# q and k heads transposed in pairs in float32 and split on the way out of PSUM; dilated groups projected in class order

## The chip, the core and the metric

The kernel runs on one core of one Trainium2 chip. The metric is the device time of one execution in microseconds. Three runs of the kernel before took 1957.49, 1953.87 and 1952.23 us: median 1953.87 us. The engines are PE (TensorE, with its weight loads shown apart as PEld), DVE (VectorE), ACT (ScalarE), POOL (GpSimd) and SP (SyncE, which here only issues DMAs).

## What is computed

Two layers of a decoder trunk over 512 tokens with 1024 features. In each layer the normed residual goes through one wide projection, which feeds four mixers of attention (A: sparse by an indexer's top 128, B: dilated windows in three groups, C: latent attention, D: a banded window with sinks); each mixer's output is gated, projected and summed, and added to the residual. What the change touches is the way from the projection to the attention of A, B and D:

```
qa = rms_norm(a_q.reshape(shp_a), qk_gain_a[l, 0])
ka = rms_norm(a_k.reshape(shp_a), qk_gain_a[l, 1])
...
B_GROUPS = ((128, 1), (512, 4), (2048, 16))
...
def to_sub(t):
    t = t.reshape(b, sub_len, dil, h, dh).transpose(0, 2, 1, 3, 4).reshape(b * dil, sub_len, h, dh)
...
s = jnp.einsum('bnqkgd,bnskd->bnkgqs', qb, kb, preferred_element_type=jnp.float32) * dh ** -0.5
```

Each head of q and of k (64 features) is divided by its root mean square over the features and multiplied by a gain. Groups 1 and 2 of mixer B attend among tokens of the same residue mod 4 (a "class" of 128 tokens) or mod 16. All of it is float32 in the reference.

## The kernel before

**Exact products.** Matmuls take `F32R` operands, which hold a rounded part of a float32. So each operand is two tiles, `hi` (a rounded copy) and `lo` (the rest), and each product is three passes: hi by hi, hi by lo, lo by hi. Weights stream through SP in slots of up to 128x768 (L402), ACT makes `hi` (L405) and DVE `lo` (L411).

**Projection.** `t_bank` fills one PSUM bank with 128 tokens by the columns of a pair of heads: for 8 tiles of the contraction 3 passes each (L512, L513, L514), 24 matmuls; the stationary operand is the activation (128x128), the moving one the weights. `f_bank` gives features by 512 tokens, with the weights stationary (L536 to L538), 512 columns a matmul.

**A pair of heads** (`do_pair`; 4 in A, 12 in B per layer, of which 8 are of groups 1 and 2, `perm`; `do_d` makes one such pair in `d0` and six more q heads in `d1`, from one normed bank of 384 columns per token tile). For each of four token tiles: a bank of 384 columns (q, k, v of two heads); v is split from PSUM into `vv`; `norm_qk` copies q and k out (`evac`, L642), squares (ACT L651), sums (DVE L653), takes the power -1/2 (POOL L378, L379), multiplies (DVE L657), applies the product of both gains to k (POOL L659), and writes `hi` (POOL L660) and `lo` (DVE L661) of each head side by side, 128 columns of F32R. After two token tiles `q_out` and `k_out` transpose each head by itself (L676, L689: 4 q and 4 k transposes of 128x128, in F32R), so that `hi` comes to lie in 64 partitions over `lo` in the other 64, and ACT copies them to the feature-major tiles `uq` and `kk(h, 0)` (L680 to L696). `k_swap` (L701, L702) then has four DMAs, issued by POOL, make `kk(h, 1)` with `lo` over `hi`. A score block is one matmul of 128 partitions with each of the two.

**Class order.** Pairs of groups 1 and 2 need their tokens sorted by class. Before, q and k are projected in token order (banks of 256 columns) and sorted by ACT as it copies them out of the transposes (L680, L693 write with a step of 128 elements). v is projected apart as one `f_bank` of 24 matmuls of 512 columns, sorted in ACT's copy to `vp` (L734), transposed back by four float32 transposes (L737) and split.

**Order of work.** `PLAN` lists pieces (pairs, attentions, gate projections `z`, merges) in order of preference; a list scheduler fixes each engine's order from it, so that banks of later pieces fill PE while an attention waits. Each engine then runs its list strictly in order. At the start, SP also writes the bias tables: `gdram` (L338), and from it copies in DRAM (`make_skew`, L347) that later loads (L372) read shifted.

Of the kernel before, what the change touches and what calls it, by code (L numbers as in the profile page):

```python
# [112 lines left out]
def plan():  # L113
    """The order of a layer's work; what comes first is preferred where several pieces are ready."""
# [127 lines left out]
def build(ctx, tc, A, depth=2, dump=None):  # L242
# [132 lines left out]
    def rsqrt(eng, r, ss, n, scale, eps=EPS):  # L375
        """r = 1 / sqrt(ss * scale + eps) on [128, n]."""
# [5 lines left out]
    def layer(l, xt):  # L382
# [8 lines left out]
        gv = lay[:, 728:920].rearrange("p (i d) -> p i d", i=3)  # L391
        sy.dma_start(pk, A["pk"][l][:, :PK])
# [22 lines left out]
        def gain_parts():  # L415
            """x * gain as hi and lo per row tile: the first products need not wait for the norm."""
# [50 lines left out]
        pg = T([128, 512], F32, "tmp")[:, :384].rearrange("p (i j d) -> p i j d", i=3, j=2)  # L467
        with tc.issue_after(wdma[0].ins):
            sy.dma_start(pg.rearrange("p i j d -> p (i j d)"), A["pk"][l][:, PK:])
        ve.scalar_tensor_tensor(gv, pg[:, :, 0], A_SC, pg[:, :, 1], op0=OP.mult, op1=OP.mult)  # L470
# [33 lines left out]
        def t_bank(slots, w, t, c0=0, c1=None, x=None):  # L504
            c1 = w if c1 is None else c1
# [25 lines left out]
        def f_bank(parts, mh, ml, w=S):  # L531
            """parts: (hi, lo) stationary views [128, 128] per row tile; moving operands mh, ml: [128, w] each."""
# [11 lines left out]
        def split_ps(hi, lo, src, scale=None):  # L544
            """hi + lo = src (* scale), src in PSUM."""
# [92 lines left out]
        def evac(o, n, scale=1.0):  # L638
            """A copy of a bank's first n columns, so that the bank is free before the norms are known."""
# [7 lines left out]
        def norm_qk(o, t, x, gi, scale=1.0):  # L647
            """o: two heads of q and of k in PSUM; hi and lo of the normed ones to x[:, t], [128, 4, 2, 64]."""
            o = evac(o, 256, scale)
            sq = T([128, 512], F32, "ssq")[:, :256]  # L650
            ac.activation(sq, o, AF.Square)  # L651
            ss = T([128, 8], F32, "nss")[:, :4]
            ve.tensor_reduce(ss, sq.rearrange("p (h d) -> p h d", h=4), axis=AX.X, op=OP.add)  # L653
            r = T([128, 8], F32, "nr")[:, :4]
            rsqrt(gp, r, ss, 4, 1.0 / 64)
# [13 lines left out]
        def q_out(uq, qx, hf, h0, n, perm):  # L669
            """Heads of qx [128, 2, n, 2, 64] (half hf of the tokens) to uq[:, h0:h0 + n], feature-major."""  # L670
            for i0 in range(0, n, 2):
                m = min(2, n - i0)
                p = ps_t(F32R)
                for i in range(m):
                    for t in range(2):
                        pe.transpose(p[:, (2 * i + t) * 128:(2 * i + t + 1) * 128], qx[:, t, i0 + i], idr)  # L676
                src = p[:, :m * 256].rearrange("p (h s) -> p h s", h=m)
                if perm:
                    dst = uq[:, h0 + i0:h0 + i0 + m].rearrange("p h (c i) -> p h i c", c=4)[:, :, hf * 64:hf * 64 + 64]
                    ac.copy(dst, src.rearrange("p h (i c) -> p h i c", c=4))  # L680
                else:
                    ac.copy(uq[:, h0 + i0:h0 + i0 + m, hf * 256:hf * 256 + 256], src)

        def k_out(kk, x, hf, perm):
            """The two k heads of x (half hf of the tokens), hi on top of lo, to kk(h, 0)."""
            p = ps_t(F32R)
            for i in range(2):
                for t in range(2):
                    pe.transpose(p[:, (2 * i + t) * 128:(2 * i + t + 1) * 128], x[:, t, 2 + i], idr)  # L689
            for i in range(2):  # L690
                src = p[:, i * 256:(i + 1) * 256]
                if perm:
                    ac.copy(kk(i, 0).rearrange("p (c i) -> p i c", c=4)[:, hf * 64:hf * 64 + 64],  # L693
                            src.rearrange("p (i c) -> p i c", c=4))
                else:
                    ac.copy(kk(i, 0)[:, hf * 256:hf * 256 + 256], src)  # L696
# [10 lines left out]

        def do_pair(job):
# [5 lines left out]
            vv = u4().rearrange("p a b -> p (a b)").rearrange("p (t h d) -> p t h d", t=NT, h=2)  # L714
            for t in range(NT):
                if t % 2 == 0:
                    x = T([128, 2, 4, 2, 64], F32R, "qk")
                o = t_bank(slots, 384, t, 0, 256 if perm else 384)
                if not perm:
                    v = o[:, 256:384].rearrange("p (h d) -> p h d", h=2)  # L720
                    split_ps(vv[:, t, :, 0:64], vv[:, t, :, 64:128], v)
                last = norm_qk(o, t % 2, x, int(br == BR_B))
                if br == BR_B:
                    topk_after(last, TOPK_B[job[2]])
                if t % 2:
                    q_out(uq, x, t // 2, 0, 2, perm)
                    k_out(kk, x, t // 2, perm)
            k_swap(kk)
            if perm:
                o = f_bank([(slots[k // 2][0][:, (k % 2) * 384 + 256:(k % 2) * 384 + 384],  # L730
                             slots[k // 2][1][:, (k % 2) * 384 + 256:(k % 2) * 384 + 384]) for k in range(KT)],
                           xhs, xls)
                vp = T([128, 512], F32, "tmp")
                ac.copy(perm_view(vp, True), nat_view(o, True))  # L734
                p = ps_t()
                for t in range(NT):
                    pe.transpose(p[:, t * 128:(t + 1) * 128], vp[:, t * 128:(t + 1) * 128], idf)  # L737
                pv = p.rearrange("p (t h d) -> p t h d", t=NT, h=2)
                split_ps(vv[:, :, :, 0:64], vv[:, :, :, 64:128], pv)
# [589 lines left out]
```

## Time and profile before

| | |
|---|---|
| median of three runs | 1953.87 us |
| the profiled execution, its span | 1949.2 us |
| PE busy | 1884.5 us, 97% |
| DVE, ACT, POOL busy | 68%, 57%, 37% |
| mean granted TensorE clock | 0.986 of full speed |
| matmuls | 11348 |

The span is that of one profiled execution, from its first to its last instruction; the medians are of whole executions, 4.7 us longer. PE is busy nearly throughout, by a measure in which matmuls overlap: a matmul's own time runs from its start to the end of its results, and the next starts well before. What a matmul costs PE is therefore the distance between starts in a stretch without waits, and that is what the timeline rows below are for. A group's mean in the rows by line is the longer, overlapping time.

### The profile page before, as it was taken

Reading aid. Unit: us, or ns where it says so; the run is one execution under the profiler, and the core shown is the slowest. Engines: PE = TensorE matmul, PEld = TensorE weight load, DVE = VectorE, ACT = ScalarE, POOL = GpSimd, SP = SyncE. Lnnn points to the kernel's source line nnn. Section 1 sums busy time; section 2 is a strip of 40 time slices with the busy share of each in tenths; the row PEclk is TensorE's granted clock in tenths of the full one; section 3 lists DMA queues with packets and bytes.
Section 4 is the critical chain, followed back from the end, with each engine's and each line's share of the span. In section 5 each row is a group of like instructions: output and inputs, shape, how many; then the busy total and the mean of one; then the engine's idle time right before and its main releaser. Section 6 shows DMA issues by size and latency. Waiting matters only on the chain.

```text
span 1949.2 us, 33221 instructions
## 1 busy us (share of the span) xinstructions
PE 1884.5 (97%) x11348; PEld 1695.6 (87%) x11348; DVE 1331.1 (68%) x3410; ACT 1103.0 (57%) x2650; POOL 728.5 (37%) x1186
## 2 busy tenths in 40 slices
PE   8759999999989999999999999999999999999999
PEld 7648889989878998998889988899899989898887
DVE  7649777758476866665469888676768686766542
ACT  6538666656455565554347776566555656555431
POOL 3615353424233346640005345253343343755000
PEclk9879999999989999999999999999999999999999
DMA  4223233342334243332252222233333333333233
GB/s 163 84 91 95 67 90 103 105 113 88 110 105 118 80 121 105 99 98 82 91 187 85 82 66 93 74 88 83 94 105 113 101 101 91 117 96 101 80 92 108
DMA packets 103420, 193.47 MB, mean 99 GB/s; under 512 B 21510, under 2 KB 35924, under 8 KB 103252
## 3 DMA queue, kind: packets, MB, share of 16 engines
q1 hardware_dynamic: 92372, 173.52, 29.4%
q0 software_dynamic: 10880, 17.83, 4.2%
q8 instruction: 90, 1.47, 0.3%
q14 instruction: 78, 0.64, 0.1%
HBM read 168.84 MB, written 12.83 MB: 93 GB/s over the span
## 4 chain that ended last, share of the span: by engine, by line
PE 88%; DMA 4%; DVE 2%; ACT 2%; POOL 2%; issue 1%; SPq 1%; DVEq 0%; ACTq 0%; POOLq 0%
PE acc L537 14%; PE acc L536 14%; PE acc L538 14%; PE acc L512 9%; PE acc L513 9%; PE acc L514 9%; PE S L923 4%; PE T L994 3%; PE T L1014 2%; DMA cbuf<-wall 1%; DMA sd<-st 1%; PE T L1033 1%; PE T L1026 1%; PE T L676 1%; PE T L689 1%
## 5 line engine op out<-in xcount | busy, mean ns | idle before, releaser
L411 DVE TENSOR_TENSOR cbufr<-cbuf,cbufr 128x768 fp32r<-128x768 f32 (+3 forms) x396 | 357.6, 906 | 140.5 <-ACT cbufr L405 139.0
L405 ACT CAST cbufr<-cbuf 128x768 fp32r<-128x768 f32 (+3 forms) x396 | 304.9, 774 | 262.4 <-PE acc L537 195.9
L513 PE MATMUL acc<-cbufr 128*128 128x384 f32 (+1 forms) x1152 | 365.8, 318 | 0.0
L512 PE MATMUL acc<-cbufr 128*128 128x384 f32 (+1 forms) x1152 | 364.1, 317 | 0.0
L514 PE MATMUL acc<-cbufr 128*128 128x384 f32 (+1 forms) x1152 | 363.9, 316 | 0.0
L536 PE MATMUL acc<-cbufr 128*128 128x512 f32 x896 | 354.5, 396 | 0.9 <-ACT raw L642 0.9
L538 PE MATMUL acc<-cbufr 128*128 128x512 f32 x896 | 353.9, 395 | 0.0
L537 PE MATMUL acc<-cbufr 128*128 128x512 f32 x896 | 353.6, 395 | 0.0
L513 PEld LDWEIGHTS acc<-cbufr 128*128 128x128 f32 x1152 | 218.7, 190 | 3.0 <-issue 1.1
L512 PEld LDWEIGHTS acc<-cbufr 128*128 128x128 f32 x1152 | 218.5, 190 | 2.7 <-ACT U L696 0.7
L514 PEld LDWEIGHTS acc<-cbufr 128*128 128x128 f32 x1152 | 218.7, 190 | 2.3 <-issue 0.8
L379 POOL TENSOR_TENSOR nr<-nx,cbuf 128x4 f32<-128x4 f32 (+2 forms) x200 | 211.6, 1060 | 11.1
L538 PEld LDWEIGHTS acc<-cbufr 128*128 128x128 f32 x896 | 168.9, 188 | 34.0
L536 PEld LDWEIGHTS acc<-cbufr 128*128 128x128 f32 x896 | 169.0, 189 | 32.7 <-ACT raw L642 1.3
L537 PEld LDWEIGHTS acc<-cbufr 128*128 128x128 f32 x896 | 169.1, 189 | 32.3 <-issue 0.7
L958 POOL TENSOR_SCALAR P<-P,rd 128x128 f32<-128x128 f32 x192 | 117.3, 621 | 195.4 <-DVE rd L956 136.2
L378 POOL TENSOR_SCALAR nx<-nss 128x4 f32<-128x4 f32 (+2 forms) x200 | 62.3, 311 | 272.2 <-DVE nss L653 243.1
L701 POOL DMA_DIRECT2D U<-U x68 | 39.3, 578 | 311.4 <-ACT U L693 190.4
L547 ACT CAST PT<-T 128x128 fp32r<-128x128 f32 (+2 forms) x224 | 102.9, 478 | 64.0 <-PE T L994 38.0
L548 DVE TENSOR_TENSOR PT<-T,PT 128x128 fp32r<-128x128 f32 (+2 forms) x224 | 119.8, 548 | 22.0 <-ACT PT L547 20.3
L945 ACT ACTIVATE P<-P,nm 128x128 f32<-128x128 f32 x192 | 101.9, 533 | 57.4 <-DVE nm L942 56.7
L642 ACT COPY raw<-acc 128x256 f32<-128x256 f32 (+2 forms) x192 | 70.4, 377 | 107.9 <-PE acc L514 74.9
(256 smaller groups left out, 3954.0 us busy)
## 6 DMA issues: line engine op xcount, KB each, us to landing
cbuf<-wall SPq DMA_DIRECT2D x284, 384.0 KB
cbuf<-wall SPq DMA_DIRECT2D x96, 256.0 KB
U<-U POOLq DMA_DIRECT2D x136, 128.0 KB, 2.8
bias<-skew SPq DMA_DIRECT2D x32, 128.0 KB
bias<-skew SPq DMA_DIRECT2D x16, 256.0 KB
skew<-gdram SPq DMA_DIRECT2D x8, 384.0 KB
cbuf<-wall SPq DMA_DIRECT2D x8, 328.0 KB
skew<-gdram SPq DMA_DIRECT2D x4, 640.0 KB
```

Of the source, the lines that this page charges most:

```text
L379: gp.tensor_tensor(r, y, mhalf[:, :n], op=OP.pow)
L405: pin(ac.copy(h, raw))
L411: pin(e.tensor_tensor(lo, raw, h, op=OP.subtract))
L512: mm(o[:, :c1 - c0], x[kt][:, 0, ts], h[:, a + c0:a + c1], start=kt == 0, stop=False)
L513: mm(o[:, :c1 - c0], x[kt][:, 0, ts], lo[:, a + c0:a + c1], start=False, stop=False)
L514: mm(o[:, :c1 - c0], x[kt][:, 1, ts], h[:, a + c0:a + c1], start=False, stop=kt == KT - 1)
L536: mm(o[:, :w], h, mh[kt], start=kt == 0, stop=False)
L537: mm(o[:, :w], h, ml[kt], start=False, stop=False)
L538: mm(o[:, :w], lo, mh[kt], start=False, stop=kt == n - 1)
L547: ac.copy(hi, src)
L548: ve.tensor_tensor(lo, src, hi, op=OP.subtract)
L958: gp.tensor_scalar(p[:, off:off + nk * 128], p[:, off:off + nk * 128], rd[:, qb:qb + 1], 0.0, op0=OP.mult, op1=OP.add)
```

## The change

**Transposes.** `norm_heads` replaces `norm_qk`: it stops at the multiplied float32 heads `qn` (tile `qh`). After all four token tiles, `heads_out` transposes two heads at once in float32 (L664 of the changed kernel: `qn` of 128 tokens by 2x64 features is one 128x128 transpose), four transposes into one bank, and splits each head's 64 partitions from PSUM: ACT writes `hi`, DVE writes `lo`. For head 0 `hi` lies in partitions 0 to 63 and `lo` in 64 to 127, for head 1 the other way round. k goes first, with its gain as a scale per partition in that split; then `k_swap`; then q. The gain is now a column of `par` (`gk`), computed from the small parameter tile, so POOL's multiplication L659, the DMA L469 of replicated gains and POOL's `hi` L660 are gone. Per pair there are 8 transposes in place of 16; in `d1` 12 in place of 24.

**Class order.** For groups 1 and 2 the stationary operand of `t_bank` is `xperm`: every fourth token of the activation, so a bank holds one class. All three of q, k and v come from banks of 384 columns; the `f_bank` for v, `vp`, its transposes, and ACT's sorting copies are gone. The stationary operand is then read with a step of 4 elements (16 bytes) between columns, in 1536 matmuls.

**Else.** `qn` has 4 buffers in place of 6, a new tag `qh` has 6; the scratch of DMAs that POOL issues is set to 4096.

```diff
-        def norm_qk(o, t, x, gi, scale=1.0):
-            """o: two heads of q and of k in PSUM; hi and lo of the normed ones to x[:, t], [128, 4, 2, 64]."""
-            o = evac(o, 256, scale)
...
-            qn = T([128, 256], F32, "qn").rearrange("p (h d) -> p h d", h=4)
...
-            (gp if GAIN_POOL else ve).tensor_tensor(qn[:, 2:4], qn[:, 2:4], gv[:, gi, None].to_broadcast([128, 2, 64]), op=OP.mult)
-            gp.tensor_scalar(x[:, t, :, 0], qn, 1.0, 0.0, op0=OP.mult, op1=OP.add)
-            return ve.tensor_tensor(x[:, t, :, 1], qn, x[:, t, :, 0], op=OP.subtract)
+        def norm_heads(o, n, scale=1.0):
+
+            o = evac(o, n * 64, scale)
...
+            qn = T([128, 512], F32, "qh")[:, :n * 64].rearrange("p (h d) -> p h d", h=n)
+            ins = ve.tensor_tensor(qn, o.rearrange("p (h d) -> p h d", h=n), r[:, :, None].to_broadcast([128, n, 64]),
+                                   op=OP.mult)
+            return qn, ins
+
+        def heads_out(dst, qns, h0, gain=None):
+
+
+            p = ps_t()
+            for t in range(NT):
+                pe.transpose(p[:, t * 128:(t + 1) * 128], qns[t][:, h0:h0 + 2].rearrange("p h d -> p (h d)"), idf)
+            for h in range(2):
+                a, b = (slice(0, 64), slice(64, 128)) if h == 0 else (slice(64, 128), slice(0, 64))
+                d = dst(h)
+                split_ps(d[a], d[b], p[a], None if gain is None else gain[a])
...
+        xperm = [xhl[:, :, kt].rearrange("p e (i c) -> p e c i", c=4) for kt in range(KT)]
...
+                xs = [xperm[kt][:, e, t] if perm else x[kt][:, e, ts] for e in range(2)]
+                mm(o[:, :w], xs[0], h[:, a:a + w], start=kt == 0, stop=False)
+                mm(o[:, :w], xs[0], lo[:, a:a + w], start=False, stop=False)
+                mm(o[:, :w], xs[1], h[:, a:a + w], start=False, stop=kt == KT - 1)
...
             for t in range(NT):
-                if t % 2 == 0:
-                    x = T([128, 2, 4, 2, 64], F32R, "qk")
-                o = t_bank(slots, 384, t, 0, 256 if perm else 384)
-                if not perm:
-                    v = o[:, 256:384].rearrange("p (h d) -> p h d", h=2)
-                    split_ps(vv[:, t, :, 0:64], vv[:, t, :, 64:128], v)
-                last = norm_qk(o, t % 2, x, int(br == BR_B))
+                o = t_bank(slots, 384, t, perm=perm)
+                v = o[:, 256:384].rearrange("p (h d) -> p h d", h=2)
+                split_ps(vv[:, t, :, 0:64], vv[:, t, :, 64:128], v)
+                qn, last = norm_heads(o, 4)
+                qns.append(qn)
...
-                if t % 2:
-                    q_out(uq, x, t // 2, 0, 2, perm)
-                    k_out(kk, x, t // 2, perm)
+            heads_out(lambda h: kk(h, 0), qns, 2, gk[:, int(br == BR_B):int(br == BR_B) + 1])
             k_swap(kk)
-            if perm:
-                o = f_bank([(slots[k // 2][0][:, (k % 2) * 384 + 256:(k % 2) * 384 + 384],
...
-                vp = T([128, 512], F32, "tmp")
-                ac.copy(perm_view(vp, True), nat_view(o, True))
...
+            heads_out(lambda h: uq[:, h], qns, 0)
             return uq, ks, vv
```

The scheduler's lists move with it. The first place is in PE's list, at the pair of group 2 and the first two heads of mixer B in layer 0: each row is a line, an operation, its output tile and its operands, and xN counts repeats. `acc` is a bank, `T` a bank of transposes or of an attention's output, `U` a tile of q, k or v, `S` scores, `qk` and `qh` the normed heads. Before, PE at the end of that pair's banks:

```order
L514 MATMUL acc_4623<-cbufr 128x256
L512 MATMUL acc_4623<-cbufr 128x256
L971 MATMUL S_4377<-U_984_4131,U_983_4130 128x256 x2
L971 MATMUL S_4386<-U_984_4131,U_983_4130 128x256 x2
L513 MATMUL acc_4623<-cbufr 128x256
L514 MATMUL acc_4623<-cbufr 128x256
L536 MATMUL acc_4683<-cbufr 128x512
L537 MATMUL acc_4683<-cbufr 128x512
L538 MATMUL acc_4683<-cbufr 128x512
```

and the same place now:

```order
L925 MATMUL S_4273<-U_961_4033,U_959_4031 128x256 x2
L510 MATMUL acc_4458<-cbufr 128x384
L511 MATMUL acc_4458<-cbufr 128x384
L512 MATMUL acc_4458<-cbufr 128x384
L534 MATMUL acc_4619<-cbufr 128x512
L535 MATMUL acc_4619<-cbufr 128x512
L536 MATMUL acc_4619<-cbufr 128x512
```

`acc_4683` is the bank of v alone, 24 matmuls of 512 columns; it is gone, the banks of q, k and v are 384 wide, and what follows them (`acc_4619`, a merge) is work that both kernels do. Later in PE's list, the transposes of that same pair, before:

```order
L1026 MATMUL T_4446<-PT_4438,U_986_4133 64x128
L676 MATMUL T_4566<-cbufr,qk_4479 128x128 x4
L689 MATMUL T_4572<-cbufr,qk_4479 128x128 x2
L1026 MATMUL T_4446<-PT_4438,U_986_4133 64x128 x11
L689 MATMUL T_4572<-cbufr,qk_4479 128x128 x2
L676 MATMUL T_4666<-cbufr,qk_4579 128x128 x4
L689 MATMUL T_4672<-cbufr,qk_4579 128x128 x4
L512 MATMUL acc_4915<-cbufr 128x384
```

and now:

```order
L980 MATMUL T_4299<-PT_4291,U_962_4034 64x128
L664 MATMUL T_4500<-cbuf,qh_4369 128x128
L664 MATMUL T_4500<-cbuf,qh_4411 128x128
L664 MATMUL T_4500<-cbuf,qh_4453 128x128
L664 MATMUL T_4500<-cbuf,qh_4495 128x128
L980 MATMUL T_4299<-PT_4291,U_962_4034 64x128 x11
L664 MATMUL T_4513<-cbuf,qh_4369 128x128
L664 MATMUL T_4513<-cbuf,qh_4411 128x128
L664 MATMUL T_4513<-cbuf,qh_4453 128x128
L664 MATMUL T_4513<-cbuf,qh_4495 128x128
```

Sixteen transposes became eight, k's four ahead of q's four, and they still stand inside the previous pair's last products of probabilities and v (L1026, now L980). The last place is SP's list at the start, where the bias tables are made. Before:

```order
L347 DMA skew_0_600<-gdram 256x1x384
L338 DMA gdram<-th_597 41x480
L347 DMA skew_2_602<-gdram 256x1x384
L347 DMA skew_4_1051<-gdram 256x1x384
L402 DMA cbuf<-wall 128x512
L372 DMA bias_1301<-skew_0_600 128x256
L372 DMA bias_1366<-skew_0_600 128x256
L372 DMA bias_1473<-skew_2_602 128x256
L347 DMA skew_6_1053<-gdram 256x1x384
L347 DMA skew_0_1470<-gdram 256x1x384
L347 DMA skew_0_1642<-gdram 256x1x256
L402 DMA cbuf<-wall 128x512 x2
```

and now:

```order
L338 DMA gdram<-th_595 41x480
L347 DMA skew_0_598<-gdram 256x1x384
L347 DMA skew_2_600<-gdram 256x1x384
L347 DMA skew_4_974<-gdram 256x1x384
L347 DMA skew_6_976<-gdram 256x1x384
L372 DMA bias_1224<-skew_0_598 128x256
L372 DMA bias_1289<-skew_0_598 128x256
L372 DMA bias_1396<-skew_2_600 128x256
L347 DMA skew_0_1393<-gdram 256x1x384
L347 DMA skew_0_1565<-gdram 256x1x256
L401 DMA cbuf<-wall 128x512 x2
```

The last write of `gdram` moved ahead of the first copy, and one load of weights moved from among the copies to before them; six copies still stand between it and the next pair of weight loads.

## Rows read from the trace of the kernel before

**Rows 1.** The page, busy us (share of the span) of each engine.
```profile
PE 1884.5 (97%) x11348; PEld 1695.6 (87%) x11348; DVE 1331.1 (68%) x3410; ACT 1103.0 (57%) x2650; POOL 728.5 (37%) x1186
```

**Rows 2.** Waits of PE: engine line <- releaser: us in total, times, longest.
```profile
PE T L803 <- DVE PT L796: 22.3, 1, 22.3
PE T L1026 <- DVE PT L548: 12.3, 3, 5.2
PE T L676 <- ACT raw L642: 11.7, 1, 11.7
```

**Rows 3.** Timeline of PE, middle of layer 0: start us, us, instruction.
```profile
646.25 0.28 PE L514 MATMUL acc<-cbufr 128*128 128x256 f32 x1
...
649.48 0.28 PE L514 MATMUL acc<-cbufr 128*128 128x256 f32 x1
...
653.01 0.39 PE L537 MATMUL acc<-cbufr 128*128 128x512 f32 x1
...
656.41 0.39 PE L537 MATMUL acc<-cbufr 128*128 128x512 f32 x1
```

**Rows 4.** Timeline of PE, a little later.
```profile
706.04 0.33 PE L512 MATMUL acc<-cbufr 128*128 128x384 f32 x1
...
709.16 0.33 PE L512 MATMUL acc<-cbufr 128*128 128x384 f32 x1
...
710.57 0.50 PE L689 MATMUL T<-cbufr,qk 128*128 128x128 f32 x4
...
711.83 0.34 PE L512 MATMUL acc<-cbufr 128*128 128x384 f32 x1
...
713.40 0.60 PE L737 MATMUL T<-cbuf,tmp 128*128 128x128 f32 x4
...
714.01 0.34 PE L513 MATMUL acc<-cbufr 128*128 128x384 f32 x1
```

**Rows 5.** PE groups by line and shape: count | busy us, mean ns.
```profile
L514 PE MATMUL acc<-cbufr 128*128 128x256 f32 x512 | 146.2, 286 | 0.0
...
L676 PE MATMUL T<-cbufr,qk 128*128 128x128 f32 x320 | 43.5, 246 | 11.7 <-ACT raw L642 11.7
...
L689 PE MATMUL T<-cbufr,qk 128*128 128x128 f32 x272 | 36.6, 249 | 0.0
...
L737 PE MATMUL T<-cbuf,tmp 128*128 128x128 f32 x64 | 9.6, 272 | 0.0
```

**Rows 6.** Weight loads (PEld) by line and shape: 128 and 64 columns.
```profile
L514 PEld LDWEIGHTS acc<-cbufr 128*128 128x128 f32 x1152 | 218.7, 190 | 2.3 <-issue 0.8 <-DVE cbufr L411 0.4
...
L1026 PEld LDWEIGHTS T<-PT,U 128*64 128x64 f32 x384 | 29.8, 140 | 17.5 <-DVE PT L548 12.8 <-ACT PT L547 3.6
```

**Rows 7.** ACT groups by line and shape.
```profile
L680 ACT CAST U<-T 128x512 fp32r<-128x512 f32 x32 | 35.5, 1111 | 21.8 <-PE T L676 21.6
...
L682 ACT CAST U<-T 128x512 fp32r<-128x512 f32 x48 | 28.1, 599 | 3.4 <-PE T L676 3.2
...
L693 ACT CAST U<-T 128x256 fp32r<-128x256 f32 x64 | 36.2, 673 | 2.4 <-PE T L689 2.3
...
L696 ACT CAST U<-T 128x256 fp32r<-128x256 f32 x72 | 23.9, 393 | 9.3 <-PE T L689 8.5 <-ACT th L1051 0.7
...
L1043 ACT COPY tmp<-T 64x512 f32<-64x512 f32 x64 | 37.2, 581 | 30.1 <-PE T L1014 21.5 <-PE T L1033 7.4
...
L1041 ACT COPY G<-T 64x512 f32<-64x512 f32 x32 | 18.5, 578 | 36.6 <-PE T L1026 35.7
```

**Rows 8.** The page, DMA issues: x count, KB each, median us to landing.
```profile
U<-U POOLq DMA_DIRECT2D x136, 128.0 KB, 2.8
```

**Rows 9.** DVE groups by line and shape.
```profile
L661 DVE TENSOR_TENSOR qk<-qn,qk 128x256 fp32r<-128x256 f32 x136 | 65.3, 481 | 15.1 <-POOL qk L660 14.9
...
L1044 DVE TENSOR_TENSOR s<-T,tmp 64x512 f32<-64x512 f32 x48 | 33.0, 688 | 34.5 <-ACT tmp L1043 34.0
```

**Rows 10.** Chain that ended last, 60 to 140 us: start us, us, what.
```profile
121.62 13.52 DMA cbuf<-wall
```

More of the change, by code (lines that the diff above doesn't have):

```diff
@@ L390, in layer @@
         r2 = lay[:, 724:728]
-        gv = lay[:, 728:920].rearrange("p (i d) -> p i d", i=3)
-        sy.dma_start(pk, A["pk"][l][:, :PK])
+        sy.dma_start(pk, A["pk"][l])
         wpos, lcnt = [0], [0.0]
@@ L466, in layer @@
         xg, sqa, idx_slots = gain_parts()
[L467 to L470, printed above, removed]
+        gk = par[:, 0:3]
+        ve.scalar_tensor_tensor(gk, pk[:, 8:14:2], A_SC, pk[:, 9:14:2], op0=OP.mult, op1=OP.mult)
         ve.memset(par[64:96, 3:4], C_SC)
@@ L502, in layer, with t_bank @@
                 ve.tensor_tensor(xl[:, 2 * i:2 * i + 2, cs], xf, hi, op=OP.subtract)
-        def t_bank(slots, w, t, c0=0, c1=None, x=None):
-            c1 = w if c1 is None else c1
+        def t_bank(slots, w, t, x=None, perm=False):
             x = x or [xhl[:, :, kt] for kt in range(KT)]
@@ L645, in evac @@
             return raw
-        def norm_qk(o, t, x, gi, scale=1.0):
-            o = evac(o, 256, scale)
-            sq = T([128, 512], F32, "ssq")[:, :256]
+        def norm_heads(o, n, scale=1.0):
+            o = evac(o, n * 64, scale)
+            sq = T([128, 512], F32, "ssq")[:, :n * 64]
             ac.activation(sq, o, AF.Square)
[L652 to L655, printed above, removed]
-            qn = T([128, 256], F32, "qn").rearrange("p (h d) -> p h d", h=4)
-            ve.tensor_tensor(qn, o.rearrange("p (h d) -> p h d", h=4), r[:, :, None].to_broadcast([128, 4, 64]),
-                             op=OP.mult)
-            (gp if GAIN_POOL else ve).tensor_tensor(qn[:, 2:4], qn[:, 2:4], gv[:, gi, None].to_broadcast([128, 2, 64]), op=OP.mult)
-            gp.tensor_scalar(x[:, t, :, 0], qn, 1.0, 0.0, op0=OP.mult, op1=OP.add)
-            return ve.tensor_tensor(x[:, t, :, 1], qn, x[:, t, :, 0], op=OP.subtract)
+            ss = T([128, 8], F32, "nss")[:, :n]
+            ve.tensor_reduce(ss, sq.rearrange("p (h d) -> p h d", h=n), axis=AX.X, op=OP.add)
+            r = T([128, 8], F32, "nr")[:, :n]
+            rsqrt(gp, r, ss, n, 1.0 / 64)
+            qn = T([128, 512], F32, "qh")[:, :n * 64].rearrange("p (h d) -> p h d", h=n)
[10 more added lines that the diff above has]
+                split_ps(d[a], d[b], p[a], None if gain is None else gain[a])
         def perm_view(x, perm):
@@ L667, in nat_view @@
             return x.rearrange("p (i c) -> p i c", c=4) if perm else x
[L669 to L677, printed above, removed]
-                if perm:
[L679 to L696, printed above, removed]
         def k_swap(kk):
@@ L706, in k_tiles, with v_tile @@
             return (a, b), lambda h, e: (a, b)[h][:, e]
+        xperm = [xhl[:, :, kt].rearrange("p e (i c) -> p e c i", c=4) for kt in range(KT)]
+        def v_tile():
+            return u4().rearrange("p a b -> p (a b)").rearrange("p (t h d) -> p t h d", t=NT, h=2)
         def do_pair(job):
@@ L713, in do_pair @@
             ks, kk = k_tiles()
-            vv = u4().rearrange("p a b -> p (a b)").rearrange("p (t h d) -> p t h d", t=NT, h=2)
+            vv = v_tile()
+            qns = []
             for t in range(NT):
-                if t % 2 == 0:
-                    x = T([128, 2, 4, 2, 64], F32R, "qk")
-                o = t_bank(slots, 384, t, 0, 256 if perm else 384)
-                if not perm:
-                    v = o[:, 256:384].rearrange("p (h d) -> p h d", h=2)
-                    split_ps(vv[:, t, :, 0:64], vv[:, t, :, 64:128], v)
-                last = norm_qk(o, t % 2, x, int(br == BR_B))
+                o = t_bank(slots, 384, t, perm=perm)
[3 more added lines that the diff above has]
+                qns.append(qn)
                 if br == BR_B:
                     topk_after(last, TOPK_B[job[2]])
-                if t % 2:
-                    q_out(uq, x, t // 2, 0, 2, perm)
-                    k_out(kk, x, t // 2, perm)
+            heads_out(lambda h: kk(h, 0), qns, 2, gk[:, int(br == BR_B):int(br == BR_B) + 1])
             k_swap(kk)
-            if perm:
-                o = f_bank([(slots[k // 2][0][:, (k % 2) * 384 + 256:(k % 2) * 384 + 384],
-                             slots[k // 2][1][:, (k % 2) * 384 + 256:(k % 2) * 384 + 384]) for k in range(KT)],
-                           xhs, xls)
-                vp = T([128, 512], F32, "tmp")
-                ac.copy(perm_view(vp, True), nat_view(o, True))
[L735 to L739, printed above, removed]
+            heads_out(lambda h: uq[:, h], qns, 0)
             return uq, ks, vv
@@ L745, in do_d @@
             ks, kk = k_tiles()
-            vv = u4().rearrange("p a b -> p (a b)").rearrange("p (t h d) -> p t h d", t=NT, h=2)
+            vv = v_tile()
+            qns = []
             for t in range(NT):
-                if t % 2 == 0:
-                    x = T([128, 2, 4, 2, 64], F32R, "qk")
                 o = t_bank(slots, 384, t, x=xg)
                 r = r2[:, t:t + 1]
-                topk_after(norm_qk(o, t % 2, x, 2, r), TOPK_D)
+                qn, last = norm_heads(o, 4, r)
+                qns.append(qn)
+                topk_after(last, TOPK_D)
@@ L753, in do_d @@
                 v = o[:, 256:384].rearrange("p (h d) -> p h d", h=2)
                 split_ps(vv[:, t, :, 0:64], vv[:, t, :, 64:128], v, r)
-                if t % 2:
-                    q_out(uqs[0], x, t // 2, 0, 2, False)
-                    k_out(kk, x, t // 2, False)
+            heads_out(lambda h: kk(h, 0), qns, 2, gk[:, 2:3])
             k_swap(kk)
+            heads_out(lambda h: uqs[0][:, h], qns, 0)
             slots = [next_slot(("d1",)) for _ in range(4)]
             uqs += [u4() for _ in range(3)]
-            for t in range(NT):
-                if t % 2 == 0:
-                    xa, xb = T([128, 2, 4, 2, 64], F32R, "qk"), T([128, 2, 4, 2, 64], F32R, "qk")
-                    qxs = [xa[:, :, 0:2], xa[:, :, 2:4], xb[:, :, 0:2]]
-                o = evac(t_bank(slots, 384, t), 384)
-                sq = T([128, 512], F32, "ssq")[:, :384]
-                ac.activation(sq, o[:, :384], AF.Square)
-                ss = T([128, 8], F32, "nss")[:, :6]
-                ve.tensor_reduce(ss, sq.rearrange("p (h d) -> p h d", h=6), axis=AX.X, op=OP.add)
-                r = T([128, 8], F32, "nr")[:, :6]
-                rsqrt(gp, r, ss, 6, 1.0 / 64)
-                for i in range(3):
-                    qn = T([128, 256], F32, "qn")[:, :128].rearrange("p (h d) -> p h d", h=2)
-                    ve.tensor_tensor(qn, o[:, i * 128:(i + 1) * 128].rearrange("p (h d) -> p h d", h=2),
-                                     r[:, 2 * i:2 * i + 2, None].to_broadcast([128, 2, 64]), op=OP.mult)
-                    gp.tensor_scalar(qxs[i][:, t % 2, :, 0], qn, 1.0, 0.0, op0=OP.mult, op1=OP.add)
-                    ve.tensor_tensor(qxs[i][:, t % 2, :, 1], qn, qxs[i][:, t % 2, :, 0], op=OP.subtract)
-                    if t % 2:
-                        q_out(uqs[i + 1], qxs[i], t // 2, 0, 2, False)
@@ L780, in do_d @@
+            qns = [norm_heads(t_bank(slots, 384, t), 6)[0] for t in range(NT)]
+            for i in range(3):
+                heads_out(lambda h: uqs[i + 1][:, h], qns, 2 * i)
             return uqs, ks, vv
@@ L1288, in host_arrays @@
     a["wall"] = wall
-    pk = np.zeros((depth, 128, PK + 384), np.float32)
+    pk = np.zeros((depth, 128, PK), np.float32)
     for l in range(depth):
@@ L1294, in host_arrays @@
             for j in range(2):
-                p[:, PK + (2 * i + j) * 64:PK + (2 * i + j + 1) * 64] = g[nm][l, j]
+                p[:, 8 + 2 * i + j] = np.tile(g[nm][l, j], 2)
         c = g["qk_gain_c"][l]
@@ L1320 @@
     arrays = host_arrays(inputs)
-    nc = bacc.Bacc("TRN2", target_bir_lowering=False, num_devices=1)
+    nc = bacc.Bacc("TRN2", target_bir_lowering=False, num_devices=1, dynamic_dma_scratch_size=4096)
     aps = {k: nc.dram_tensor(k, v.shape, mybir.dt.from_np(v.dtype), kind="ExternalInput").ap() for k, v in arrays.items()}
```

3 lines of the change are left out of this document (removed), and 2 rows, old and new, of the table BUFS.

## Prediction

> **What bounds the kernel now.** I read the engines' busy shares first: PE 97%, DVE 68%, ACT 57%, POOL 37% [rows 1]. Then PE's waits, because a busy PE could still be a PE that is fed late: two waits of 11.7 and 22.3 us at the start of layer 0 and 12.3 us in three waits in mixer B are nearly all that matters [rows 2]. So for some 1,880 us the end of the kernel is set by how many matmuls PE has and what each costs it, and the change has to be priced in distances between the starts of matmuls. The timeline gives these in stretches without waits [rows 3, 4]:
>
> - 256 columns: 27 matmuls from 646.25 to 649.48, 0.1196 us each.
> - 512 columns: 15 from 653.01 to 656.41, 0.2267 us.
> - 384 columns: 18 from 706.04 to 709.16, 0.1733 us.
> - F32R transposes: 12 (three rows of four) start at 710.57. The first matmul behind a group of transposes starts its successor late, so I count to the second one, at 711.83, and take one usual distance off: 711.83 - 710.57 - 0.173 = 1.09 us, 0.0906 each.
> - float32 transposes: four from 713.40, the second matmul behind them at 714.01: 0.61 - 0.173 = 0.437 us, 0.109 each.
>
> A float32 transpose is thus dearer than one in F32R, but not twice as dear.
>
> **The change part by part.** *Transposes of q and k.* Before there are 320 + 272 = 592 in F32R [rows 5]: 17 pairs of 16 and 24 in `d1`, per layer. After there are half, 296, in float32. 592 x 0.0906 = 53.6 us go, 296 x 0.109 = 32.3 us come: -21.3 us. All of it lies on PE, hence on the path.
>
> *Transposes of v.* 64 float32 ones go [rows 5]: 64 x 0.109 = -7.0 us.
>
> *Banks of the 16 class pairs.* Before, each has 96 matmuls of 256 columns (16 x 96 = 1536, 512 for each of three lines [rows 5]) and 24 of 512 columns: 1536 x 0.1196 + 384 x 0.2267 = 183.7 + 87.1 = 270.8 us. After, 1536 of 384 columns: 266.2 us if they cost what 384 columns cost now. The columns are the same in number; only the fixed part of 384 matmuls is saved: -4.6 us. Here the condition is large, and it is the crux: the weights of these 1536 matmuls are read with a step of 16 bytes, and no matmul of the kernel before does that. Today a weight load runs beside the previous matmul and is hidden: from its 190 ns for 128 columns and 140 for 64 [rows 6] it takes (190 - 140)/64 = 0.78 ns per column, 100 ns for 128, well under 173. The nearest rows to a stepped read point two ways. ACT reads PSUM with a step of 512 bytes for 32 copies in 578 ns where unstepped copies of that size take 581 [rows 7]: a step on the reading side costs nothing. But ACT's writes into SBUF with such a step take 1111 and 673 ns for 512 and 256 columns against 599 and 393 [rows 7]: per column (1111 - 673)/256 = 1.71 ns against (599 - 393)/256 = 0.80, 2.13 times. So the load is between 100 and 100 x 2.13 = 213 ns. Below 173 it stays hidden and the price is 0; at 213 the load is the bound, and each matmul costs 213 - 173 = 40 ns more, or 53 if the 13 ns that 384 columns now take beyond 384/2.4 = 160 ns (the granted clock is the full 2.4 GHz there) come on top: 1536 x 0.040 to 0.053 = +61 to +81 us. I take 0, by the row that reads as PE does; the other end is in the range.
>
> [...]
>
> *Work on other engines.* DVE loses 136 subtractions at 481 ns (65 us) and gains 148 splits of 64x512 from PSUM, at 688 ns if they cost what L1044 does [rows 9]: 102 us. With v's splits DVE ends some 35 us higher, at about 70%. ACT loses its stepped copies, POOL two passes per token tile. None of that is near PE's 97%, so I price it at nothing; what hides it is the work of other pairs that stands in PE's list between a pair's banks and its transposes.
>
> *Chain to the scores.* k's halves reach `k_swap` after a DVE pass more than before (688 ns); the swap lands 2.8 us after issue [rows 8]. In PE's list k's transposes now stand first, and some 6 us or more of banks stand between them and the first score in all but a few pairs. Price 0; uncovered it is a rival.
>
> *Start of layer 0.* The 22.3 us wait ends when weights land that SP could issue only behind six copies of bias tables: 13.52 us from 121.62 [rows 10]. The new SP list keeps six copies ahead of that pair of loads. What D's share of the transposes saves before that point, 40 x 0.0906 - 20 x 0.109 = 1.4 us, becomes wait. The 11.7 us wait may vanish, but only into the 22.3.
>
> Sum: -21.3 - 7.0 - 4.6 + 1.4 = -31.5 us on the span, 1949.2 - 31.5 = 1917.7. Whole runs are longer than the span: the median is 1953.9, 4.7 above it. Forecast **1922 us**, 1.6% faster.
>
> **The rivals.** *The weight load becomes the bound (slower).* Mechanism and price as above: 1536 loads of 213 ns in place of hidden ones, +61 to +81 us, net +30 to +50: 1984 to 2004, say 1994 us. It decides from a load of about 173 + 31.5/1.536 = 194 ns; between 173 and 194 the change still gains. [...] Against it: ACT's stepped reads, and 73 ns of room under the matmul. [...]
>
> *The handover comes late.* Before, each class pair had v's bank, 24 x 0.2267 = 5.4 us, behind its q and k banks; now the eight transposes wait for the fourth tile's norm, and POOL's four swaps per pair share a smaller scratch, so that an issue may wait for an earlier swap to land, 2.8 us. If PE waits 0.5 to 1.4 us (one to two DVE passes) at each of 34 pairs: +17 to +48 us, 1940 to 1970, say 1950 us. Against it: scores wait for those DMAs almost nowhere now, PE's list has distance, and POOL is nearly idle afterwards.
>
> *More than the count.* The 12.3 us of waits in B and some of those at the start dissolve, since POOL and ACT are freer: 1922 - 12 = about 1908 us. For it: DVE's wait for POOL's `hi` goes. Against it: these waits end in DVE, which gets more work, and in DMAs that nothing speeds up.
>
> **How the numbers follow.** Forecast 0.48, weight load 0.36, late handover 0.09, more 0.07. About 0.3% (6 us) is what a measurement can tell from no change. Faster takes the forecast, the last rival and a quarter of the handover and partial loads: 0.58. Slower takes most of the weight load: 0.34. The same: 0.08. The forecast's own range is 1910 to 1937 (waits of 12 us coming or going). The 8-in-10 range must reach into the second sign: 1910 to 1998, which leaves out half of the last rival and the far end of the first.
>
> **What would show it.** Right: 10,600 matmuls or so, 296 transposes of `qh` at 0.109 us, class banks at 0.173 us between starts, PE's waits still led by the start. Wrong by the load: weight loads of class banks well over 190 ns and starts over 0.21 us apart, everything else as forecast. Wrong by the handover: waits of PE for `U` from DMA or for L664's operands, repeated per pair. The forecast falls if class banks cost more than 0.194 us a matmul.

## Result and profile after: 3.7% slower

The changed kernel takes 2026.0 us against 1953.1 us (the median with a fourth run of the kernel before), a ratio of 1.037 (1.035 to 1.038): slower, where 1922 us and a gain had been forecast, and above the range's end of 1998. The page's first rows, span and busy time of each engine:

```profile
span 2026.5 us, 31220 instructions
...
PE 1955.2 (96%) x10604; PEld 1776.5 (88%) x10604; DVE 1387.8 (68%) x3430; ACT 1069.5 (53%) x2614; POOL 552.3 (27%) x890
```

Against [rows 1], 744 matmuls are gone and PE is nevertheless busy 70.7 us longer. Its idle time, span less busy, went from 64.7 to 71.3 us. So 70.7 of the +77.3 us of span lie in what the matmuls cost and 6.6 in waiting. PE's waits (engine, line, releaser: us in total, times, longest) answer to [rows 2]:

```profile
PE T L757 <- DVE PT L750: 34.2, 1, 34.2
PE T L980 <- DVE PT L546: 13.3, 2, 10.0
...
PE T L948 <- POOL P L912: 2.3, 3, 1.3
```

The two waits at the start, 22.3 and 11.7 us, have become one of 34.2, and the wait in mixer B is 13.3 us, about as it was. No wait for the new transposes' operands (L664) stands among them; all 296 have 0.1 us of idle time before them.

The timeline of PE (start us, us, instruction) in a bank of a class pair, layer 0, answers to [rows 3, 4]:

```profile
343.07 0.40 PE L512 MATMUL acc<-cbufr 128*128 128x384 f32 x1
343.30 0.40 PE L510 MATMUL acc<-cbufr 128*128 128x384 f32 x1
343.54 0.40 PE L511 MATMUL acc<-cbufr 128*128 128x384 f32 x1
...
349.84 0.40 PE L511 MATMUL acc<-cbufr 128*128 128x384 f32 x1
```

From 343.07 to 349.84 there are 29 intervals: 0.2334 us a matmul, where 384 columns took 0.1733. The clock is not the cause; the view by windows (us, busy time of PE, PEld, DVE, ACT and POOL, granted clock, DMA share, GB/s) has it at 1.00 of full speed:

```profile
343.07:349.84 6.77, 6.77 (x31) 6.77 (x30) 3.59 (x6) 3.28 (x7) 3.21 (x6) 1.00 0.64 171
```

The weight loads (PEld) where a class bank is followed by a bank of `f_bank` (L534 to L536, contiguous) show why:

```profile
391.24 0.33 PEld L511 LDWEIGHTS acc<-cbufr 128*128 128x128 f32 x1
391.47 0.33 PEld L512 LDWEIGHTS acc<-cbufr 128*128 128x128 f32 x1
391.71 0.21 PEld L534 LDWEIGHTS acc<-cbufr 128*128 128x128 f32 x1
391.90 0.19 PEld L535 LDWEIGHTS acc<-cbufr 128*128 128x128 f32 x1
392.13 0.19 PEld L536 LDWEIGHTS acc<-cbufr 128*128 128x128 f32 x1
```

The stepped loads of L511 and L512 are recorded with 0.33 us, the contiguous ones of L535 and L536 with 0.19, as in [rows 6]. The recorded time holds more than a load takes of PE, since matmuls of 256 columns start 0.1196 us apart behind loads recorded with 0.19; the 0.14 us more are the step's. Per group:

```profile
L511 PEld LDWEIGHTS acc<-cbufr 128*128 128x128 f32 x1152 | 288.6, 251 | 2.4 <-issue 1.0
...
L535 PEld LDWEIGHTS acc<-cbufr 128*128 128x128 f32 x768 | 145.5, 189 | 27.3
```

The 1152 loads of L511 mix 512 stepped and 640 contiguous ones, hence 251 ns between the two.

### The profile page after: what moved, and what is told of

It is laid out like the page before. It is cut to its first block, busy times and chain, and to the rows that moved or that the text cites. A ratio compares the mean times of both kernels' runs of the same rounds, so it can differ in the third digit from the quotient of the medians.

```text
span 2026.5 us, 31220 instructions
## 1 busy us (share of the span) xinstructions
PE 1955.2 (96%) x10604; PEld 1776.5 (88%) x10604; DVE 1387.8 (68%) x3430; ACT 1069.5 (53%) x2614; POOL 552.3 (27%) x890
## 4 chain that ended last, share of the span: by engine, by line
PE 87%; DMA 3%; DVE 3%; ACT 2%; SPq 2%; issue 1%; POOL 1%; ACTq 0%; POOLq 0%; DVEq 0%
PE acc L534 13%; PE acc L535 13%; PE acc L536 12%; PE acc L510 11%; PE acc L512 11%; PE acc L511 11%; PE S L877 3%; PE T L948 3%; PE T L968 2%; DMA cbuf<-wall 2%; PE T L664 1%; SPq L347 1%; PE T L980 1%; PE T L987 1%; DMA sd<-st 1%
## 5 line engine op out<-in xcount | busy, mean ns | idle before, releaser
L510 PE MATMUL acc<-cbufr 128*128 128x384 f32 x1152 | 424.6, 369 | 0.8 <-DVE U L546 0.4
L512 PE MATMUL acc<-cbufr 128*128 128x384 f32 x1152 | 424.6, 369 | 0.0
L511 PE MATMUL acc<-cbufr 128*128 128x384 f32 x1152 | 423.4, 368 | 0.0
L534 PE MATMUL acc<-cbufr 128*128 128x512 f32 x768 | 305.5, 398 | 1.7 <-DVE PT L546 1.5
L535 PE MATMUL acc<-cbufr 128*128 128x512 f32 x768 | 304.3, 396 | 0.0
L536 PE MATMUL acc<-cbufr 128*128 128x512 f32 x768 | 303.8, 396 | 0.0
L510 PEld LDWEIGHTS acc<-cbufr 128*128 128x128 f32 x1152 | 287.8, 250 | 4.0 <-PE S L607 1.5
L512 PEld LDWEIGHTS acc<-cbufr 128*128 128x128 f32 x1152 | 288.3, 250 | 3.1 <-issue 1.7
L511 PEld LDWEIGHTS acc<-cbufr 128*128 128x128 f32 x1152 | 288.6, 251 | 2.4 <-issue 1.0
L534 PEld LDWEIGHTS acc<-cbufr 128*128 128x128 f32 x768 | 145.6, 190 | 29.7 <-DVE PT L546 1.9
L912 POOL TENSOR_SCALAR P<-P,rd 128x128 f32<-128x128 f32 x192 | 108.3, 576 | 231.0 <-DVE rd L910 145.9
L536 PEld LDWEIGHTS acc<-cbufr 128*128 128x128 f32 x768 | 145.3, 189 | 28.4
L535 PEld LDWEIGHTS acc<-cbufr 128*128 128x128 f32 x768 | 145.5, 189 | 27.3
L680 POOL DMA_DIRECT2D U<-U x68 | 37.9, 557 | 431.4 <-ACT U L548 406.4
L549 DVE SCALAR_TENSOR_TENSOR U<-T,cbuf,U 64x512 fp32r<-64x512 f32 (+1 forms) x100 | 66.1, 662 | 79.7 <-ACT U L548 78.2
```

The source lines that it names most:

```text
L510: mm(o[:, :w], xs[0], h[:, a:a + w], start=kt == 0, stop=False)
L511: mm(o[:, :w], xs[0], lo[:, a:a + w], start=False, stop=False)
L512: mm(o[:, :w], xs[1], h[:, a:a + w], start=False, stop=kt == KT - 1)
L534: mm(o[:, :w], h, mh[kt], start=kt == 0, stop=False)
L535: mm(o[:, :w], h, ml[kt], start=False, stop=False)
L536: mm(o[:, :w], lo, mh[kt], start=False, stop=kt == n - 1)
```

## Experiments

**Theory 1** was formed from these rows: a weight load with a step of 16 bytes takes 0.2333 us of PE and is the bound of its matmul, whatever the matmul's width. The main rival: the loss comes from the order of work or from late handovers, and the wide spacing goes with it. Two runs take the step away and put it alone, two change a size beside it; the other three ask where else such a step costs something.

**The step taken away.**

```diff
-                o = t_bank(slots, 384, t, perm=perm)
+                o = t_bank(slots, 384, t)
```

> The changed kernel, but the banks of the pairs of groups 1 and 2 take their 128 tokens in token order, weights contiguous, 384 columns as in the changed kernel; that part of the result is therefore of other tokens than the reference's. Theory 1 (the stepped weight load sets the distance between matmuls): in the changed kernel these 1536 matmuls start 0.2333 us apart; contiguous ones of 384 columns 0.1733, so 1536 x 0.060 = 92 us go and the time is 2026 - 92 = 1934 us, weight loads all near 190 ns. Rival (the loss is elsewhere: late handovers, DVE's splits, the order of work): it stays above 1990 us.

Measured: 1931.8 us, 0.989 (0.987 to 0.990) of before. PE is busy 97.1 us less than in the changed kernel, and 26.4 less than before:

```profile
span 1930.5 us, 31220 instructions
...
PE 1858.1 (96%) x10604; PEld 1677.2 (87%) x10604; DVE 1385.0 (72%) x3430; ACT 1068.7 (55%) x2614; POOL 556.0 (29%) x890
```

Theory 1 gave 1934, the rival above 1990. The weight loads of L510 to L512 are back at a mean of 188 ns. The step alone turns a gain of 1.1% into a loss of 3.7%.

**The step put alone** into the kernel before, in its 256-column banks of q and k:

```diff
-            ts = slice(t * 128, (t + 1) * 128)
+            ts = slice(t * 128, (t + 1) * 128) if c1 - c0 == w else slice(t, 512, 4)
```

> The kernel before, with the one edit that the 256-column banks of q and k of groups 1 and 2 read their weights with the step of 4 elements (the sorting copies stay, so q and k of these pairs come out in another token order than the reference's). Theory 1, load-bound: each of 1536 matmuls costs 0.2333 us in place of 0.1196, +175 us, 2128 us. Rival, 60 ns added to each: +92 us, 2046 us. Rival, the changed order of work is needed for the loss: 1954 us.

Measured: 2124.5 us, 1.087 (1.085 to 1.089) of before, where theory 1 gave 2128. The timeline:

```profile
342.83 0.40 PE L512 MATMUL acc<-cbufr 128*128 128x256 f32 x1
343.06 0.40 PE L513 MATMUL acc<-cbufr 128*128 128x256 f32 x1
...
352.17 0.40 PE L513 MATMUL acc<-cbufr 128*128 128x256 f32 x1
```

40 intervals from 342.83 to 352.17 are 0.2335 us each, for 256 columns that took 0.1196 [rows 3]. That is the same distance as with 384 columns: the moving columns no longer matter. The rival that adds 60 ns to each matmul (2046) falls, and so does the one that needs the new order of work (1954).

**More columns under the same load.** In `t_bank` of the class pairs:

```diff
-                a = (kt % 2) * w
+                a = (kt % 2) * (256 if perm else w)
+                n = 512 if perm else w
...
```

> The changed kernel, with 512 moving columns instead of 384 in the stepped banks (128 columns that nobody reads, and weights shifted for half of the contraction tiles, so q, k and v of these pairs are other numbers). Theory 1, load-bound: a stepped load takes 0.2333 us of PE, more than 512 contiguous columns (0.2267), so a third more columns are free: 2026 us, within 6. Rival, the load no longer overlaps and adds 60 ns to whatever the columns cost: 0.2267 + 0.060 = 0.287 us each, 1536 x 0.053 = +82, 2108 us.

Measured: 2033.7 us, 1.041 (1.039 to 1.042) of before, 7.7 us above the changed kernel, where theory 1 gave 6 at most and the rival 82. In the timeline 21 intervals are 0.2352 us each, 1.8 ns more than with 384 columns:

```profile
344.83 0.40 PE L512 MATMUL acc<-cbufr 128*128 128x512 f32 x1
345.07 0.39 PE L513 MATMUL acc<-cbufr 128*128 128x512 f32 x1
...
349.77 0.39 PE L512 MATMUL acc<-cbufr 128*128 128x512 f32 x1
```

So theory 1's bound of 6 us is passed by 1.7. Between the two profiled executions the span differs by 2.9 us (2029.4 and 2026.5) and PE's busy time by 2.8, which is 1536 x 1.8 ns; the rest of the 7.7 lies between executions of one kernel (2031.2 to 2035.6 us here, 2025.4 to 2028.3 in the changed kernel). 128 columns more in each of 1536 matmuls are nearly free, since the load covers them. The rival that adds 60 ns falls.

**Which steps cost.** Each of the eight tiles of the contraction reads with another step, from its own line (L502 with step 1, then 2, 3, 4, 5, 8, 16, and L523 with 32):

```diff
+            n = (1, 2, 3, 4, 5, 8, 16, 32)[kt]
+            return flat[:, e, t:t + 127 * n + 1:n]
...
```

> The changed kernel, whose stepped banks read each of the eight contraction tiles with another step: 1, 2, 3, 4, 5, 8, 16 and 32 elements of 4 bytes, each from a line of its own (192 loads each); q, k and v of these pairs are therefore other numbers. [...] Theory 1b, the price grows with the distance: 2 lies near 235 ns, 8 and more lie above 330, matmuls of steps 8 to 32 start more than 0.233 us apart, and the time is above 2026 us.

Weight loads by line, with mean ns of one:

```profile
L517 PEld LDWEIGHTS acc<-cbufr 128*128 128x128 f32 x192 | 53.5, 337 | 0.1
L514 PEld LDWEIGHTS acc<-cbufr 128*128 128x128 f32 x192 | 51.2, 321 | 1.1 <-issue 1.0
L511 PEld LDWEIGHTS acc<-cbufr 128*128 128x128 f32 x192 | 50.8, 323 | 0.7 <-issue 0.7
L523 PEld LDWEIGHTS acc<-cbufr 128*128 128x128 f32 x192 | 50.5, 321 | 0.0
L520 PEld LDWEIGHTS acc<-cbufr 128*128 128x128 f32 x192 | 49.9, 320 | 0.0
...
L508 PEld LDWEIGHTS acc<-cbufr 128*128 128x128 f32 x192 | 39.4, 254 | 0.0
L505 PEld LDWEIGHTS acc<-cbufr 128*128 128x128 f32 x192 | 34.9, 195 | 0.5 <-issue 0.5
L502 PEld LDWEIGHTS acc<-cbufr 128*128 128x128 f32 x192 | 34.8, 193 | 1.4 <-issue 0.5
```

Steps 1 and 2 take 193 and 195 ns, step 3 (L508) 254, steps 4, 5, 16 and 32 all 320 to 323, step 8 (L517) 337. So the price grows up to a step of 16 bytes and not beyond it: theory 1b falls. The rows fit a price set by how many elements lie in the same 16 bytes: with two or more there is no price, with one the full price, and step 3, which leaves two in some and one in others, lies between. A price that rises from 8 to 16 bytes of distance and then stays flat would give the same rows; no run here tells the two apart. In the trace, matmuls of steps 1, 2 and 3 start 175, 174 and 178 ns apart (medians within a line), those of steps 4, 5, 16 and 32 229 to 237, those of step 8 246. So step 3's longer load is still hidden by 384 columns, and three of the eight tiles cost nothing: 3/8 x 92 = 35 us, where the time, 1989.9 us in one run, lies 36 us under the changed kernel.

With the step of 4 elements, one in 16 bytes, a load of 128 columns takes 0.2334 us of PE, the distance measured in the changed kernel.

**A version without the step that keeps the rest.** Class pairs project as before (q and k in 256 columns in token order, v by `f_bank`), and the sorting becomes a stepped read of PSUM in the split of the paired transposes:

```diff
+        def class_in(x, perm):
+            return x.rearrange("p (i c) -> p c i", c=4) if perm else x
...
-                split_ps(d[a], d[b], p[a], None if gain is None else gain[a])
+                split_ps(class_out(d[a], perm), class_out(d[b], perm), class_in(p[a], perm),
+                         None if gain is None else gain[a])
```

> The changed kernel's paired float32 transposes, with the class order made elsewhere: pairs of groups 1 and 2 project q and k in token order (256 columns) and v as features by tokens, as in the kernel before, and the sorting is a stepped read of PSUM in the two passes that split the transposes. From the run in token order (1931.8 us): the banks cost 270.8 us in place of 266.2 and the 64 transposes of v come back, +4.6 + 7.0 = 1943 us, 0.5% under before. It tells whether the transposes alone gain: theory 1 (the step was the only loss) 1943, within 5; rival (eight transposes behind four norms are late where v's bank follows them, or ACT and DVE read stepped PSUM slowly enough to hold PE) 1953 or more.

Measured: 1933.0 us, 0.989 (0.988 to 0.991) of before: it lies under both kernels, and 10 us under the 1943 expected, outside the 5 that theory 1 allowed; the rival's 1953 falls. Page and the three longest waits of PE:

```profile
span 1932.5 us, 32010 instructions
...
PE 1868.6 (97%) x11052; PEld 1673.1 (87%) x11052; DVE 1382.0 (72%) x3382; ACT 1087.9 (56%) x2582; POOL 531.1 (27%) x890
```

```profile
PE T L775 <- DVE PT L768: 34.4, 1, 34.4
PE acc L525 <- ACT cbufr L404: 6.4, 1, 6.4
PE S L943 <- DMA U<-U: 4.4, 4, 1.7
```

Compared with the run in token order, PE is busy 10.5 us longer, close to the 11.6 priced (4.6 + 7.0), but idle 8.5 us less: the wait of mixer B for DVE's `PT`, 13.3 us in the changed kernel and 15.5 in the run in token order, is not there. In the run in token order it was:

```profile
PE T L980 <- DVE PT L546: 15.5, 3, 12.4
```

Why this order of work avoids it is open; v's bank alone is not the reason, since the kernel before had that bank and the wait too [rows 2]. The stepped reads of PSUM cost nothing. ACT's copies to `hi` of 64x512 and DVE's subtractions to `lo`, first in this kernel, where 32 of the 80 read with a step, then in the run in token order, where none do:

```profile
L546 ACT CAST U<-T 64x512 fp32r<-64x512 f32 x80 | 46.0, 582 | 12.7 <-DVE U L547 9.6 <-PE T L665 1.8
L547 DVE TENSOR_TENSOR U<-T,U 64x512 fp32r<-64x512 f32 x80 | 54.7, 688 | 6.1 <-ACT U L546 4.0
```

```profile
L545 ACT CAST U<-T 64x512 fp32r<-64x512 f32 x80 | 46.0, 582 | 14.0 <-DVE U L546 11.4 <-PE T L664 1.3
L546 DVE TENSOR_TENSOR U<-T,U 64x512 fp32r<-64x512 f32 x80 | 54.7, 689 | 6.0 <-ACT U L545 3.3
```

The means are 582 ns in both kernels for ACT, 688 and 689 for DVE.

**The step on the moving side.** Here v's bank reads its 512 moving columns in class order:

```diff
-                           xhs, xls)
+                           [class_in(x, True) for x in xhs], [class_in(x, True) for x in xls])
...
```

> As the kernel that sorts in the split, with one edit: v's 384 matmuls of 512 columns in groups 1 and 2 read the moving activation in class order, a step of 4 elements, so that ACT's copy out of that bank needs no sorting. [...] Theory b, only weight loads pay: 1943 us.

Had the moving operand paid the 0.2333 / 128 = 1.82 ns a column of the weights, 512 columns would have taken 0.93 us in place of 0.2267, and the time would have been 384 x 0.71 = 271 us above 1943, 2214 us. Measured, in one run: 2017.2 us, between that and theory b's 1943. The timeline of such a bank, with transposes a little later:

```profile
360.24 0.66 PE L535 MATMUL acc<-cbufr 128*128 128x512 f32 x1
360.70 0.66 PE L536 MATMUL acc<-cbufr 128*128 128x512 f32 x1
...
363.93 0.66 PE L537 MATMUL acc<-cbufr 128*128 128x512 f32 x1
...
368.27 0.60 PE L665 MATMUL T<-cbuf,qh 128*128 128x128 f32 x4
368.62 0.36 PE L513 MATMUL acc<-cbufr 128*128 128x256 f32 x1
368.82 0.28 PE L511 MATMUL acc<-cbufr 128*128 128x256 f32 x1
```

Eight intervals from 360.24 to 363.93: 0.461 us for 512 columns in place of 0.227, or 0.90 ns a column. 384 x 0.234 = 90 us; measured were 84. So the moving operand pays too, but half as much a column as the weights (0.2334 / 128 = 1.82 ns). Neither 2214 us nor theory b's 1943 held.

**The step on ACT and DVE.** The weights' casts read SBUF with the step:

```diff
-            pin(ac.copy(h, raw))
+            rs = raw.rearrange("p (b a) -> p a b", a=4)
+            pin(ac.copy(h.rearrange("p (a b) -> p a b", a=4), rs))
...
```

> The kernel that sorts in the split, with the casts of the weights (ACT's copy to hi, DVE's subtraction to lo) reading the loaded weights in SBUF with a step of 4 elements and writing without one; the weights' columns are therefore in another order and the results other numbers. It asks whether the row on which the choice of 0 rested (ACT's stepped reads of PSUM cost nothing) would have held for SBUF. [...]

The author's estimate, if a column with a step in SBUF costs ACT and DVE the weight load's 1.82 ns: 768 columns take ACT 768 x 1.82 = 1.40 us in place of 836 ns, which for 284 casts is 160 us, DVE gains about as much, and the time rises by 20 to 160 us. If the step costs nothing, as in PSUM, ACT's 836 and DVE's 962 ns stay, 1933 us. Rows of ACT's cast and of DVE's subtraction, by shape, first the kernel that sorts in the split:

```profile
L404 ACT CAST cbufr<-cbuf 128x768 fp32r<-128x768 f32 x284 | 236.3, 836 | 162.8 <-PE acc L536 134.4 <-DMA cbuf<-wall 14.5 <-PE acc L527 6.5
L404 ACT CAST cbufr<-cbuf 128x512 fp32r<-128x512 f32 x96 | 59.4, 620 | 109.6 <-PE acc L536 63.9 <-DMA cbuf<-wall 39.9 <-issue 2.2
```

```profile
L410 DVE TENSOR_TENSOR cbufr<-cbuf,cbufr 128x768 fp32r<-128x768 f32 x284 | 271.0, 962 | 80.5 <-ACT cbufr L404 78.4 <-issue 0.3
L410 DVE TENSOR_TENSOR cbufr<-cbuf,cbufr 128x512 fp32r<-128x512 f32 x96 | 74.1, 774 | 84.9 <-ACT cbufr L404 73.5 <-PE T L665 6.9 <-ACT U L549 2.7
```

then with the step:

```profile
L405 ACT CAST cbufr<-cbuf 128x768 fp32r<-128x768 f32 x284 | 445.5, 1591 | 67.9 <-PE acc L538 40.6 <-DMA cbuf<-wall 13.8 <-PE acc L529 5.0
L405 ACT CAST cbufr<-cbuf 128x512 fp32r<-128x512 f32 x96 | 107.2, 1121 | 76.9 <-DMA cbuf<-wall 39.4 <-PE acc L538 35.4 <-issue 1.2
```

```profile
L411 DVE TENSOR_TENSOR cbufr<-cbuf,cbufr 128x768 fp32r<-128x768 f32 x284 | 439.6, 1556 | 99.7 <-ACT cbufr L405 95.4 <-PE acc L539 3.8
L411 DVE TENSOR_TENSOR cbufr<-cbuf,cbufr 128x512 fp32r<-128x512 f32 x96 | 110.6, 1155 | 73.6 <-ACT cbufr L405 71.4 <-PE acc L539 1.2 <-PE T L1007 0.5
```

ACT's column costs (1591 - 1121)/256 = 1.84 ns, against (836 - 620)/256 = 0.84; DVE's (1556 - 1155)/256 = 1.57, against 0.73. The whole took 2028.9 us in one run, 96 us more than the kernel that sorts in the split, inside the 20 to 160; ACT is busy 241 and DVE 200 us longer, where about 160 each had been estimated for the 768 columns alone. The 836 and 962 ns became 1591 and 1556, so the step in SBUF is not free. ACT pays what the weight load pays: 1.84 ns a column against 1.82. DVE, with one of its two inputs stepped, pays less, 1.57, and the moving operand half, 0.90.

## Why the prediction was wrong

*Class banks: the failed step.* Their condition was named as the crux, both ends stood there, and I took 0 "by the row that reads as PE does". That row, ACT's L1041 in [rows 7], reads PSUM; the weights lie in SBUF. The casts show that the same ACT pays 2.2 times per column for a step of 16 bytes in SBUF (1.84 ns against 0.84), and the split shows that PSUM asks nothing for it (582 ns both ways). The likeness that counted was the memory, not the direction. The term was -4.6 us; at 0.2334 us it is 1536 x 0.2334 - 270.8 = +87.7.

*The first rival: right mechanism, too small.* Its load of 213 ns came from ACT's stepped writes (2.13 x 100 ns); the distance measured is 233, so the price was 60 ns a matmul, 92 us, not 61 to 81. The 81 rests on 160 ns for 384 columns, from a clock of 2.4 GHz that no view gives; [rows 3] give (0.2267 - 0.1196)/256 = 0.418 ns a column, 161 ns for 384. Its point of decision, 0.194 us, was passed by far. Its time, 1994, has 71 us for the load and was 32 us short: 21 by the price, the rest by the base below and by what stays open at the end.

*Transposes of q and k: right.* There are 296 of them, and in the timeline of the stepped moving operand four of them (there L665) start at 368.27 and the second matmul behind them at 368.82: 0.55 - 0.12 = 0.43 us with the 256 columns of [rows 3], 0.108 each, where 0.109 had been priced. Counted so over the whole traces, group by group and without recorded waits, the 592 before take 57.9 us and the 296 take 35.3 in the run in token order, 33.2 in the version that sorts in the split: -22.6 and -24.7 against -21.3. That version has them as the main saving on PE; PE is busy only 15.9 us less there, so some 9 us come back in other matmuls, which stays open; the time falls by 19.3.

*The base, 1917.7 of span, was 12.8 us too low.* The run in token order has all of the sum without the step, and its span is 1930.5. Some 3 us of the difference come from which executions were profiled: every measured time here is 1.7 to 1.9 us above its own span, so the 4.7 us between span and median was no general distance, and the execution with the span 1949.2 was a short one. In the medians the forecast of 1922 stands against 1931.8. In the spans, half of the difference is idle time of PE: 72.4 us against 64.7, +7.7 where +1.4 was forecast, 6.3 us. The other half is busy time: -26.4 where the terms add to -32.9, 6.5 us. No single term explains this, and the cause stays open.

*Other engines, scores, start: right.* DVE's busy time rose by 57 us, more than the 35 forecast, but it is 68% busy and not the bound. The waits at the start merged into 34.2 us, as said. *Late handover* did not come: in the changed kernel PE is idle 0.1 us in all before L664's transposes. That an issue of a swap waits for an earlier one to land was not shown: POOL's idle time before L679 that the trace puts down to no releaser is 6.5 us in 35 times, 0.2 at most, and before L680 there is none. *More than the count* fell: the wait in B stayed in the changed kernel.

From the changed kernel's +77.3 us of span: +92.3 from the step (1536 x 0.0601), -31.5 of forecast, +12.8 of base, together +73.6; 3.7 us are not accounted for. The medians, 72.9 us apart, put the step at 2026.0 - 1931.8 = 94.2 us.

## What to carry to other kernels

When a view changes an operand's step, ask first in which memory it lies and how many elements it leaves in 16 bytes: in this kernel two float32 were free for a weight load (195 ns against 193), and with one the load outlasted 512 moving columns (0.2352 us a matmul against 0.2267). A sort is best put where a stepped read costs nothing, here ACT's and DVE's reads of PSUM (582 ns both ways, 688 and 689). And where the likeliest value of a disputed term is chosen by the nearest row, the row has to be near in the thing that sets the price.

## What the runs showed of the hardware

A matmul behind a stepped weight load starts 0.2335, 0.2334 and 0.2352 us after the one before it with 256, 384 and 512 columns: weight load and columns overlap almost fully, and the longer one counts. Read from SBUF with a step of 16 bytes, a column takes 1.82 ns on the weights, 1.84 on ACT, 1.57 on DVE (one of two inputs stepped), but 0.90 on the moving operand. Read from PSUM with that step, it costs ACT and DVE nothing (582 ns both ways, 688 and 689). Step 8 loads slower (337 ns) than steps 4, 5, 16 and 32 (320 to 323); no run here says why.
